# The first input of a decoder trunk: transposed as it was loaded, scaled while it is split

## The chip, the cores and the metric

The kernel runs on one core of one Trainium2 chip. TensorE does matrix products and transposes, VectorE and ScalarE work on tiles of 128 partitions, GpSimd does small things, and SyncE issues most loads. The metric is the device time of one execution in microseconds (us), lower is better.

## The reference

Two layers of a decoder, 256 tokens of width 1024, all in fp32. Each sub-layer is `x <- x + w * RMSNorm(f(RMSNorm(x)))`. The change touches only the start of the first one, whose f is a SwiGLU:

```python
def rms_norm(x, g):
    xf = x.astype(jnp.float32)
    y = xf * lax.rsqrt(jnp.mean(xf * xf, axis=-1, keepdims=True) + NORM_EPS)
    return (y * g.astype(jnp.float32)).astype(x.dtype)

def swiglu(x, w_in, w_out):
    gate, up = jnp.split(x @ w_in, 2, axis=-1)
    return (jax.nn.silu(gate) * up) @ w_out
```

w_in is 1024 x 5632, w_out 2816 x 1024. Five other sub-layers follow: a combined state-space and attention mixer, a recurrent mixer and three more SwiGLUs. None of their code is changed.

## The kernel before

**Precision.** Every fp32 operand of a large product is split into a high part (rounded to the format that TensorE streams fast) and a low part (what is left), and a product is made of three: high x high, high x low, low x high. ScalarE makes the high part by a copy, VectorE the low part by a subtraction. This is done for each piece of weights (`raw` to `w`, lines 252 and 253, in `prepare`) and for the input (`xT`, line 295, in `split_to`).

**Tiling.** Tokens come in two tiles of 128 (t = 0, 1). The input stands transposed in `xT`: 8 blocks of 128 channels, each with its high and low part for 256 tokens. The hidden width of 2816 is cut into 22 columns f, each with 128 gate and 128 up channels. For f = 0, 1, 2 the products go token tile by token tile (plan entries "A", `a_tile`, 16 products each: 8 wide ones of 512, 8 narrow ones of 256), after that both tiles together ("B"). The weights of a column come in two pieces of 512 KB. Four `raw` buffers hold pieces as loaded; a load waits until VectorE has split the piece that was in its buffer.

**The start.** `first_norms` lays out the start. The factor 1/rms of a token is not applied to the input; it is applied later to the hidden columns (`rs`, lines 548, 549 and 578), so only the weight of the norm, g, must reach the input before the products. Before, g was loaded as one row (`g_row`), spread over all partitions by products with a row of ones (`gain`, line 136), multiplied with the input on VectorE (`scaled`, line 396), transposed on TensorE (`flips`, line 140) and split, four blocks at a time (line 295). Five dummy products (`WARM`) on a tile of ones go ahead. `square` (line 390) sums the squares of a token tile's half on ScalarE, and GpSimd makes 1/rms of it (lines 302, 303). Tile 0 comes first; the two halves of tile 1 are transposed within the products of the first column (`second`).

**What sets the order.** TensorE's order is that in which the code calls it. ScalarE's and VectorE's order comes from a scheduler with priorities, but in `first_norms` it is fixed by hand: `turn` makes each instruction follow the one before it on its engine, and `weights(n)` puts the splitting of the next piece of weights into that row. Semaphores are set by the framework. It also makes instructions on different engines follow each other if they touch one bank of PSUM (the memory that TensorE writes; a tile called `rot` or `side` is one bank).

Of the kernel before, what the change touches and what calls it, by code (L numbers as in the profile page):

```python
# [8 lines left out]
F32 = mybir.dt.float32  # L9
# [3 lines left out]
ALU = mybir.AluOpType  # L13
# [3 lines left out]
P = 128  # L17
# [16 lines left out]
WARM = 5  # L34
# [78 lines left out]
def hybrid_trunk(ctx: ExitStack, tc: tile.TileContext, x_in, norm_g, ffn_in, ffn_out,  # L113
                 hyb_cols, hyb_v, hyb_dtf, conv_s, bias_dtf, a_log, d_rep, ssm_g, hyb_out,
                 rec_a, rec_cols, rec_vec, rec_wa, rec_wx, rec_out, out):
# [59 lines left out]
    g_row = begin.tile([P, DM], F32, name="g_row")  # L175
    act.dma_start(g_row[0:1, :], norm_g[0, 0:1, :])
# [87 lines left out]
    def halves(dst, ps):  # L264

        tmp = work.tile([P, 256], F32, name="half", bufs=2)
        act.copy(tmp, ps[:, 256:512])  # L267
        dve.tensor_tensor(dst, ps[:, 0:256], tmp, op=ALU.add)  # L268
# [107 lines left out]
    def first_norms(xT):  # L376
# [18 lines left out]
        def scaled(t, h):  # L395
            turn(dve.tensor_tensor(xg[t][:, h, :], xs[t][:, h * 512:(h + 1) * 512], gain[h], op=ALU.mult))

        def flips(t, h):
            ps = side()
            for k in range(4):  # L400
                flip(ps[:, k * P:(k + 1) * P], xg[t][:, h, k * P:(k + 1) * P])
            return ps.rearrange("p (k c) -> p k c", k=4), [xT[:, 4 * h:4 * h + 4, j, t * P:(t + 1) * P] for j in range(2)]
# [6 lines left out]
        def second():  # L409
            for h, lag in ((0, 0.5), (1, 1.0)):  # L410
                yield lag
                ps, dst = flips(1, h)
                turn(*split_to(dst[0], dst[1], ps))
            square(1, 0)
            square(1, 1)
            weights(4)
            hold[:] = latest.values()
            normed.add((0, 1))
            norms.discard((0, 1))

# [3 lines left out]
        gain, ms = [], []  # L424
        for t in range(NT):
            ms.append(work.tile([P, 2], F32, name="ms", bufs=4))
            rs.append(work.tile([P, 1], F32, name="r", bufs=4))
        slot = wp.tile([P, NT, 2, 512], F32, name="w", bufs=8)
        xg = [slot[:, t] for t in range(NT)]
        for h in range(2):  # L430
            gain.append(rot())
            mm(gain[h], ones[0:1, :], g_row[0:1, h * 512:(h + 1) * 512], True, True)
        square(0, 0)
        scaled(0, 0)
        scaled(0, 1)
        ps, dst = flips(0, 0)
        held = split_to(dst[0], dst[1], ps)
        turn(held[0])
        scaled(1, 0)
# [651 lines left out]
```

## Time and profile before

| | |
|---|---|
| median of 3 runs | 1053.39 us (1053.22 to 1054.23) |
| the profiled execution | 1052.26 us, of which the span is 1050.5 us |
| TensorE busy | 1037.0 us, 99% of the span |
| VectorE busy | 735.1 us, 70% |
| ScalarE busy | 600.3 us, 57% |

The span is the time from the first to the last instruction that the profile shows. PE is TensorE's product, PEld its loading of the stationary operand, DVE VectorE, ACT ScalarE, POOL GpSimd, SPq and ACTq the queues from which loads are issued. A row of the order of time gives start, duration, engine, line, operation, and in brackets how long the engine had been idle and what ended that. A product on fp32 operands shows as two records.

### The profile page before, as it was taken

To read this page: it belongs to the slowest core of one execution; us is meant where nothing else is said; L and a number is where in the kernel's file an instruction comes from. 1 tells how busy PE (TensorE), PEld (TensorE's weight loads), DVE (VectorE), ACT (ScalarE), POOL (GpSimd) and SP (SyncE) were. 2 spreads that over 40 slices of the span, in tenths; PEclk is the share of its full clock that TensorE was granted. 3 is DMA by queue.
4 is the path that set the end of the run, shared out by engine and by line. 5 is a ranking of instruction groups with operands and counts; after the bars stand their busy time and mean duration, and the time that the engine had idled before them with its cause. 6 is when DMAs were issued, how large, how long until landed. Compare 5 with 4: busy or idle time off the path is not lost.

```text
span 1050.5 us, 16060 instructions
## 1 busy us (share of the span) xinstructions
PE 1037.0 (99%) x6072; PEld 911.2 (87%) x6072; DVE 735.1 (70%) x1171; ACT 600.3 (57%) x1062; POOL 40.5 (4%) x78
## 2 busy tenths in 40 slices
PE   8999999999999999999999999999999999999997
PEld 6888888899999988888888888888889888888886
DVE  6876778589888766856567685666759878655563
ACT  5764555455565565655556474555659857554551
POOL 0011101100000001000000100000010010000000
PEclk9999999999999999999999999999999999999999
DMA  6886666366545563866567286566735356765521
GB/s 215 307 259 182 199 196 193 97 221 192 187 146 167 154 201 102 294 205 182 185 200 235 81 279 202 180 193 196 234 120 182 119 183 237 226 195 202 182 81 40
DMA packets 55699, 195.77 MB, mean 186 GB/s; under 512 B 6957, under 2 KB 8133, under 8 KB 55622
## 3 DMA queue, kind: packets, MB, share of 16 engines
q1 hardware_dynamic: 52416, 189.91, 56.2%
q10 hardware_dynamic: 3206, 4.84, 1.5%
q8 instruction: 47, 0.77, 0.3%
q14 instruction: 30, 0.25, 0.1%
HBM read 193.66 MB, written 1.07 MB: 185 GB/s over the span
## 4 chain that ended last, share of the span: by engine, by line
PE 74%; DVE 8%; DMA 7%; ACT 5%; issue 3%; POOL 1%; DVEq 0%; POOLq 0%; ACTq 0%; SPq 0%
PE rot L136 47%; PE side L136 26%; DMA raw<-in_ffn_out_dram 5%; DVE w L253 4%; ACT w L252 3%; DMA raw<-in_ffn_in_dram 2%; ACT junk L314 1%; PE rot L140 1%; DVE sg L268 1%; DVE xn L330 0%; POOL r L303 0%; DVE sc L966 0%; DVE x L365 0%; DVE sg L578 0%; ACT half L267 0%
## 5 line engine op out<-in xcount | busy, mean ns | idle before, releaser
L136 PE MATMUL rot<-xT,w 128*128 128x256 f32 (+1 forms) x3512 | 571.2, 321 | 0.0
L253 DVE TENSOR_TENSOR w<-raw,w 128x1024 fp32r<-128x1024 f32 (+1 forms) x350 | 431.2, 1235 | 190.0 <-ACT w L252 188.4
L136 PEld LDWEIGHTS rot<-xT,w 128*128 128x128 f32 x3512 | 504.3, 190 | 51.3 <-issue 1.3
L252 ACT CAST w<-raw 128x1024 fp32r<-128x1024 f32 (+1 forms) x350 | 364.7, 1047 | 159.9 <-DMA raw<-in_ffn_out_dram 121.1
L136 PE MATMUL side<-w,hid 128*128 128x512 f32 x1056 | 253.9, 390 | 0.3 <-ACT hid L295 0.3
L136 PEld LDWEIGHTS side<-w,hid 128*128 128x128 f32 x1056 | 197.2, 188 | 42.0 <-ACT hid L295 0.7
L136 PE MATMUL rot<-w,xT 128*128 128x256 f32 (+1 forms) x768 | 121.3, 316 | 2.1 <-DVE w L253 1.7
L136 PEld LDWEIGHTS rot<-w,xT 128*128 128x128 f32 x768 | 106.2, 192 | 12.0 <-DVE w L253 2.5
L295 ACT CAST hid<-up 128x256 fp32r<-128x256 f32 x76 | 30.9, 406 | 105.9 <-DVE up L583 105.7
L267 ACT COPY half<-rot 128x256 f32<-128x256 f32 x176 | 63.7, 362 | 9.6 <-PE rot L136 9.2
L295 DVE TENSOR_TENSOR hid<-up,hid 128x256 fp32r<-128x256 f32 x76 | 32.2, 424 | 27.7 <-ACT hid L295 27.7
L268 DVE TENSOR_TENSOR sg<-rot,half 128x256 f32<-128x256 f32 x100 | 41.8, 418 | 9.3 <-ACT half L267 9.3
L579 ACT ACTIVATE sg<-sg 128x256 f32<-128x256 f32 x76 | 31.7, 418 | 28.9 <-DVE sg L268 16.2
L136 PE MATMUL side<-w,os 128*128 128x512 f32 x192 | 46.2, 396 | 0.0
L136 PEld LDWEIGHTS side<-w,os 128*128 128x128 f32 x192 | 35.6, 188 | 7.9
L268 DVE TENSOR_TENSOR up<-rot,half 128x256 f32<-128x256 f32 x76 | 31.8, 419 | 4.3 <-ACT half L267 4.3
L302 POOL TENSOR_SCALAR r<-ms 128x1 f32<-128x1 f32 x24 | 7.2, 300 | 699.2 <-ACT junk L314 683.8
L583 DVE TENSOR_TENSOR up<-sg,up 128x256 f32<-128x256 f32 x76 | 31.8, 418 | 2.3 <-POOL up L582 1.5
L362 DVE TENSOR_TENSOR xn<-side,g_post 128x512 f32<-128x512 f32 x24 | 16.5, 691 | 17.9 <-ACT junk L314 17.5
L330 DVE SCALAR_TENSOR_TENSOR xn<-x,r,g_pre 128x512 f32<-128x512 f32 x20 | 14.2, 749 | 16.8 <-POOL r L303 16.8
L314 ACT ACTIVATE junk<-side 128x512 bf16<-128x512 f32 x24 | 14.3, 597 | 19.6 <-PE side L136 18.7
L314 ACT ACTIVATE junk<-x 128x512 bf16<-128x512 f32 x20 | 12.6, 631 | 19.4 <-DVE x L365 19.2
(197 smaller groups left out, 540.7 us busy)
## 6 DMA issues: line engine op xcount, KB each, us to landing
raw<-in_ffn_in_dram SPq DMA_DIRECT2D x176, 512.0 KB, 4.4
raw<-in_ffn_out_dram SPq DMA_DIRECT2D x88, 512.0 KB, 4.4
raw<-in_hyb_cols_dram SPq DMA_DIRECT2D x36, 512.0 KB, 4.1
raw<-in_hyb_out_dram SPq DMA_DIRECT2D x16, 512.0 KB, 3.6
raw<-in_hyb_v_dram SPq DMA_DIRECT2D x8, 512.0 KB, 4.1
raw<-in_rec_a_dram SPq DMA_DIRECT2D x8, 512.0 KB, 4.7
raw<-in_rec_cols_dram SPq DMA_DIRECT2D x8, 512.0 KB, 4.5
raw<-in_rec_out_dram SPq DMA_DIRECT2D x8, 512.0 KB, 3.6
```

The lines of the kernel that those rows point to most:

```text
L136: pe.matmul(ps, lhsT=lhsT, rhs=rhs, start=start, stop=stop)
L140: pe.transpose(ps, src, ident)
L252: splits.append(behind(act.copy(w[:, 0, c], raw[:, c]), hold))
L253: splits.append(behind(dve.tensor_tensor(w[:, 1, c], raw[:, c], w[:, 0, c].bitcast(F32), op=ALU.subtract), hold))
L267: act.copy(tmp, ps[:, 256:512])
L268: dve.tensor_tensor(dst, ps[:, 0:256], tmp, op=ALU.add)
L295: return act.copy(hi, src), dve.tensor_tensor(lo, src, hi.bitcast(F32), op=ALU.subtract)
L314: behind(act.activation(junk, src, func=AF.Square, scale=1.0 / (32.0 * weight), accum_out=ms[:, h:h + 1]), firsts)
L330: dve.scalar_tensor_tensor(xn[h], xt[:, cols], r, state["g_pre"][:, cols], op0=ALU.mult, op1=ALU.mult)
L362: behind(dve.tensor_tensor(hg[h], acc[h], state["g_post"][:, cols], op=ALU.mult), firsts)
L579: act.activation(sg, sg, func=AF.Silu)
L583: dve.tensor_tensor(up, sg, up, op=ALU.mult)
```

## The change

The input is transposed as it was loaded, and g, now loaded as a column of 8 values per partition, is a scale of the split: ScalarE's high part is `activation(scale=g)`, VectorE's low part is `src * g - high`. Since g differs from block to block, a split takes one block (128 x 128) and no longer four at once. All 16 transposes, of both token tiles, stand in a row ahead of the first product, with eight dummy products before them and four behind them. The order on ScalarE and VectorE is written out anew, and `halves` of the first columns gets an order behind it.

```diff
-WARM = 5
+WARM = 8
...
-    g_row = begin.tile([P, DM], F32, name="g_row")
-    act.dma_start(g_row[0:1, :], norm_g[0, 0:1, :])
+    g_cols = begin.tile([P, KT], F32, name="g_cols")
+    act.dma_start(g_cols, g_first)
...
-        def scaled(t, h):
-            turn(dve.tensor_tensor(xg[t][:, h, :], xs[t][:, h * 512:(h + 1) * 512], gain[h], op=ALU.mult))
-
         def flips(t, h):
             ps = side()
             for k in range(4):
-                flip(ps[:, k * P:(k + 1) * P], xg[t][:, h, k * P:(k + 1) * P])
-            return ps.rearrange("p (k c) -> p k c", k=4), [xT[:, 4 * h:4 * h + 4, j, t * P:(t + 1) * P] for j in range(2)]
+                flip(ps[:, k * P:(k + 1) * P], xs[t][:, (4 * h + k) * P:(4 * h + k + 1) * P])
+            return ps
+
+        def parts(t, h):
+            for k in range(4):
+                n, src = 4 * h + k, turned[t, h][:, k * P:(k + 1) * P]
+                hi, lo = (xT[:, n, j, t * P:(t + 1) * P] for j in range(2))
+                turn(act.activation(hi, src, func=AF.Identity, scale=g_cols[:, n:n + 1]))
+                turn(dve.scalar_tensor_tensor(lo, src, g_cols[:, n:n + 1], hi.bitcast(F32), op0=ALU.mult, op1=ALU.subtract))
...
+        turned = {(t, h): flips(t, h) for t in range(NT) for h in range(2)}
+        for _ in range(WARM // 2):
+            mm(warm[:, 0:P], ones, ones, True, True)
         square(0, 0)
...
+        parts(0, 0)
+        weights(1, 2)
+        parts(0, 1)
+        weights(2)
+        parts(1, 0)
+        parts(1, 1)
         square(0, 1)
...
+        state["ready"] = [list(latest.values())]
+        weights(4)
+        square(1, 0)
+        square(1, 1)
...
-                halves(sg, ps)
+                halves(sg, ps, state["ready"][t] if not ph else ())
...
+        "g_first": c(a["norm_g"][0, 0].reshape(KT, P).T),
```

The first place is ScalarE, from the first square to the cast of the second column's weights. Names: `junk` is a square, `side` a bank with four transposed blocks, `w` a piece of weights, `half` the copy that closes the first column's first token tile; the brackets say which semaphores an instruction waits for. Before:

```order
L295 CAST xT_98<-side_118 128x4x128 [waits PE_49]
L390 ACTIVATE junk_126,ms_105<-x0_83 128x512 [waits Activation_49]
L252 CAST w_132<-raw_130 128x512 [waits DMAHW3_49]
L252 CAST w_132<-raw_130 128x512
L295 CAST xT_98<-side_137 128x4x128 [waits PE_49]
L252 CAST w_146<-raw_144 128x1024 [waits DMAHW4_49]
L295 CAST xT_98<-side_159 128x4x128 [waits PE_49]
L295 CAST xT_98<-side_170 128x4x128 [waits PE_49]
L390 ACTIVATE junk_177,ms_107<-x1_84 128x512 [waits DMAHW2_49,Activation_49]
L390 ACTIVATE junk_179,ms_107<-x1_84 128x512 [waits Activation_49]
L267 COPY half_202<-rot_154 128x256 [waits PE_49]
L252 CAST w_185<-raw_183 128x1024 [waits DMAHW5_49]
```

Now, from the second group of parts on (the first, `side_112`, stands ahead of the first two rows in the same way):

```order
L252 CAST w_148<-raw_146 128x512 [waits DMAHW3_49]
L252 CAST w_148<-raw_146 128x512
L405 ACTIVATE xT_98<-side_117,g_cols_81 128x128 [waits PE_49]
L405 ACTIVATE xT_98<-side_117,g_cols_81 128x128 [waits DVE_49] x3
L252 CAST w_163<-raw_161 128x1024 [waits DMAHW4_49]
L405 ACTIVATE xT_98<-side_122,g_cols_81 128x128 [waits PE_49]
L405 ACTIVATE xT_98<-side_122,g_cols_81 128x128 [waits DVE_49] x3
L405 ACTIVATE xT_98<-side_127,g_cols_81 128x128 [waits PE_49]
L405 ACTIVATE xT_98<-side_127,g_cols_81 128x128 [waits DVE_49] x3
L390 ACTIVATE junk_182,ms_108<-x0_83 128x512 [waits Activation_49]
L267 COPY half_249<-rot_231 128x256 [waits PE_49]
L252 CAST w_188<-raw_186 128x1024 [waits DMAHW5_49]
```

Each cast of four blocks became four activations, of which the last three wait for VectorE (the value waited for is the count of the low part just before); all 16 stand ahead of the copy, and the two squares of tile 1 have moved behind the last row.

The second place is VectorE in the same stretch. Before:

```order
L396 TENSOR_TENSOR w_109<-x1_84,rot_110 128x512 [waits DMAHW2_49]
L295 TENSOR_TENSOR xT_98<-side_118,xT_98 128x4x128 [waits Activation_49]
L253 TENSOR_TENSOR w_132<-raw_130,w_132 128x512 [waits DMAHW3_49,Activation_49]
L253 TENSOR_TENSOR w_132<-raw_130,w_132 128x512 [waits Activation_49]
L295 TENSOR_TENSOR xT_98<-side_137,xT_98 128x4x128 [waits Activation_49]
L253 TENSOR_TENSOR w_146<-raw_144,w_146 128x1024 [waits DMAHW4_49,Activation_49]
L396 TENSOR_TENSOR w_109<-x1_84,rot_112 128x512
L295 TENSOR_TENSOR xT_98<-side_159,xT_98 128x4x128 [waits Activation_49]
L295 TENSOR_TENSOR xT_98<-side_170,xT_98 128x4x128 [waits Activation_49]
```

Now:

```order
L406 SCALAR_TENSOR_TENSOR xT_98<-side_112,g_cols_81,xT_98 128x128 [waits DMAHW0_49,Activation_49]
L406 SCALAR_TENSOR_TENSOR xT_98<-side_112,g_cols_81,xT_98 128x128 [waits Activation_49] x3
L253 TENSOR_TENSOR w_148<-raw_146,w_148 128x512 [waits DMAHW3_49,Activation_49]
L253 TENSOR_TENSOR w_148<-raw_146,w_148 128x512 [waits Activation_49]
L406 SCALAR_TENSOR_TENSOR xT_98<-side_117,g_cols_81,xT_98 128x128 [waits Activation_49] x4
L253 TENSOR_TENSOR w_163<-raw_161,w_163 128x1024 [waits DMAHW4_49,Activation_49]
L406 SCALAR_TENSOR_TENSOR xT_98<-side_122,g_cols_81,xT_98 128x128 [waits Activation_49] x4
L406 SCALAR_TENSOR_TENSOR xT_98<-side_127,g_cols_81,xT_98 128x128 [waits Activation_49] x4
```

The multiplications by g (`w_109`, a borrowed buffer) are gone, and each low part waits for the high part of its own block.

The third place is TensorE from its first instruction to the first column's second token tile. `rot_99` is the dummies' bank, `rot_154` and later `rot_231` the first token tile's sums. Before:

```order
L136 MATMUL rot_99<-ones_87 128x128 x5
L136 MATMUL rot_110<-g_row_81,ones_87 128x512
L136 MATMUL rot_112<-g_row_81,ones_87 128x512
L140 MATMUL side_118<-ident_91,w_109 128x128 x4
L140 MATMUL side_137<-ident_91,w_109 128x128 x4
L136 MATMUL rot_154<-w_132,xT_98 128x512
L136 MATMUL rot_154<-w_132,xT_98 128x256 x2
L136 MATMUL rot_154<-w_132,xT_98 128x512
L140 MATMUL side_159<-ident_91,w_109 128x128 x4
```

Now:

```order
L136 MATMUL rot_99<-ones_87 128x128 x8
L140 MATMUL side_112<-ident_91,x0_83 128x128 x4
L140 MATMUL side_117<-ident_91,x0_83 128x128 x4
L140 MATMUL side_122<-ident_91,x1_84 128x128 x4
L140 MATMUL side_127<-ident_91,x1_84 128x128 x4
L136 MATMUL rot_99<-ones_87 128x128 x4
L136 MATMUL rot_231<-w_148,xT_98 128x512
```

The transposes read the input as it was loaded (`x0`, `x1`), and the eight that stood between the first products have moved ahead of them.

## Rows read from the trace of the kernel before

**Rows 1.** The page: busy time by engine; the chain that ended last, by engine.

```profile
PE 1037.0 (99%) x6072; PEld 911.2 (87%) x6072; DVE 735.1 (70%) x1171; ACT 600.3 (57%) x1062; POOL 40.5 (4%) x78
PE 74%; DVE 8%; DMA 7%; ACT 5%; issue 3%; POOL 1%; DVEq 0%; POOLq 0%; ACTq 0%; SPq 0%
```

**Rows 2.** Stretches: from and to, length, busy time by engine, clock, DMA.

```profile
10.89:20.04 9.15, 9.15 (x40) 7.72 (x40) 6.05 (x9) 6.13 (x12) 0.87 (x2) 1.00 0.37 115
20.04:200.00 179.96, 179.65 (x957) 154.75 (x957) 133.72 (x190) 101.95 (x174) 18.62 (x23) 1.00 0.67 211
```

**Rows 3.** Order of time, 0 to 11 us: start, duration, engine, line, operation.

```profile
1.10 2.50 PE L136 MATMUL rot<-ones 128*128 128x128 f32 x10 [1.10 <-DVE power L298]
...
3.53 3.78 PE L136 MATMUL rot<-g_row,ones 1*128 1x512 f32 x4
4.49 0.63 ACT L390 ACTIVATE junk<-x 128x512 bf16<-128x512 f32 x1 [1.66 <-DMA x<-in_x_dram]
...
7.24 1.97 PE L140 MATMUL side<-ident,w 128*128 128x128 f32 x8
...
8.39 0.58 ACT L295 CAST xT<-side 128x512 fp32r<-128x512 f32 x1 [3.18 <-PE side L140]
...
9.01 0.69 DVE L295 TENSOR_TENSOR xT<-side,xT 128x512 fp32r<-128x512 f32 x1 [0.38 <-ACT xT L295]
...
9.50 1.12 ACT L252 CAST w<-raw 128x512 fp32r<-128x512 f32 x2
...
10.14 1.29 DVE L253 TENSOR_TENSOR w<-raw,w 128x512 fp32r<-128x512 f32 x2 [0.43 <-ACT w L252]
```

**Rows 4.** Order of time, 17 to 23 us.

```profile
17.43 0.35 ACT L267 COPY half<-rot 128x256 f32<-128x256 f32 x1
...
17.68 1.05 ACT L252 CAST w<-raw 128x1024 fp32r<-128x1024 f32 x1
...
18.76 1.23 DVE L253 TENSOR_TENSOR w<-raw,w 128x1024 fp32r<-128x1024 f32 x1 [0.53 <-ACT w L252]
...
20.04 2.65 PEld L136 LDWEIGHTS rot<-w,xT 128*128 128x128 f32 x16 [0.41 <-DVE w L253]
...
22.96 2.65 PEld L136 LDWEIGHTS rot<-w,xT 128*128 128x128 f32 x16
```

**Rows 5.** Loads: KB, us to landing; then the first weights' load: ns, start, landing.

```profile
x<-in_x_dram SPq DMA_DIRECT2D x2, 512.0 KB, 4.1
...
dsk<-in_d_rep_dram ACTq DMA_DIRECT2D x1, 4.0 KB, 1.7
...
L246 SPq DMA_DIRECT2D raw<-in_ffn_in_dram x1: 423/423/423, 1.7 to 1.7; - x1
DMA to landing us min/median/max: 5.3/5.3/5.3
```

**Rows 6.** ScalarE by form: shapes, count | busy us, mean ns | idle before.

```profile
L295 ACT CAST hid<-rot 128x128 fp32r<-128x128 f32 x24 | 6.4, 272 | 0.0
...
L545 ACT ACTIVATE h<-sg 128x128 f32<-128x128 f32 x18 | 5.6, 312 | 3.8 <-DVE sg L268 3.8
...
L947 ACT ACTIVATE sc<-side,hb 128x256 f32<-128x256 f32 x8 | 4.0, 496 | 0.1
...
L877 ACT ACTIVATE th<-rot 128x256 f32<-128x256 f32 x8 | 2.9, 380 | 11.1 <-PE rot L136 11.1
...
L548 ACT ACTIVATE h<-sg,r 128x128 f32<-128x128 f32 x6 | 2.4, 401 | 1.2 <-DVE sg L268 1.2
```

**Rows 7.** VectorE by form.

```profile
L295 DVE TENSOR_TENSOR hid<-rot,hid 128x128 fp32r<-128x128 f32 x24 | 6.7, 281 | 0.0
...
L549 DVE SCALAR_TENSOR_TENSOR h<-sg,r,h 128x128 f32<-128x128 f32 x6 | 2.1, 347 | 0.3 <-ACT h L548 0.3
```

**Rows 8.** TensorE by form, 13 to 14.2 us; then 16.6 to 19.7 us.

```profile
L136 PE MATMUL rot<-w,xT 128*128 128x512 f32 x2 | 1.1, 628 | 0.0
...
L136 PE MATMUL rot<-w,xT 128*128 128x512 f32 x11 | 2.9, 393 | 0.0
```

More of the change, by code (lines that the diff above doesn't have):

```diff
@@ L114, in hybrid_trunk @@
                  hyb_cols, hyb_v, hyb_dtf, conv_s, bias_dtf, a_log, d_rep, ssm_g, hyb_out,
-                 rec_a, rec_cols, rec_vec, rec_wa, rec_wx, rec_out, out):
+                 rec_a, rec_cols, rec_vec, rec_wa, rec_wx, rec_out, g_first, out):
     nc = tc.nc
@@ L262, in slabs, with halves @@
         return [split[k] for k in keys]
-    def halves(dst, ps):
+    def halves(dst, ps, firsts=()):
         tmp = work.tile([P, 256], F32, name="half", bufs=2)
-        act.copy(tmp, ps[:, 256:512])
-        dve.tensor_tensor(dst, ps[:, 0:256], tmp, op=ALU.add)
+        behind(act.copy(tmp, ps[:, 256:512]), firsts)
+        behind(dve.tensor_tensor(dst, ps[:, 0:256], tmp, op=ALU.add), firsts)
     def mm_wide(sums, groups):
@@ L407, in weights @@
             turn(*splits)
[L409 to L419, printed above, removed]
         warm = rot()
@@ L423, in first_norms @@
             mm(warm[:, 0:P], ones, ones, True, True)
[L424 to L432, printed above, removed]
-        square(0, 0)
[L434 to L439, printed above, removed]
-        turn(held[1])
-        square(0, 1)
-        weights(1, 2)
-        ps, dst = flips(0, 1)
-        turn(*split_to(dst[0], dst[1], ps))
-        weights(2)
-        scaled(1, 1)
-        normed.add((0, 0))
-        norms.add((0, 1))
+        ms = [work.tile([P, 2], F32, name="ms", bufs=4) for _ in range(NT)]
+        rs.extend(work.tile([P, 1], F32, name="r", bufs=4) for _ in range(NT))
+        turned = {(t, h): flips(t, h) for t in range(NT) for h in range(2)}
+        for _ in range(WARM // 2):
+            mm(warm[:, 0:P], ones, ones, True, True)
+        square(0, 0)
+        parts(0, 0)
[4 more added lines that the diff above has]
+        parts(1, 1)
+        square(0, 1)
+        state["ready"] = [list(latest.values())]
+        weights(4)
+        square(1, 0)
+        square(1, 1)
+        state["ready"].append(list(latest.values()))
+        hold[:] = latest.values()
+        normed.update({(0, 0), (0, 1)})
         start_pool.__exit__(None, None, None)
-        spawn(second())
     rs = []
```

## The prediction

> **What bounds the kernel now.** I read the page's first and fourth parts first. TensorE is busy for 99% of the span, and the chain that ended last lies on it for 74% [rows 1]. So a microsecond counts only if TensorE starts its dense work earlier or later, or waits inside it. The second view is TensorE's busy time by stretch: from 20.04 to 200 us it is 179.65 of 179.96 us [rows 2]. Behind 20.04 us this phase has almost nothing to gain, and almost no slack that could swallow a delay; what TensorE waits in later phases is for work that follows its own products and moves with it. The third view is the order of time up to 23 us [rows 3, 4]. Up to 20.04 us TensorE does five dummy products, the products that spread the norm's weight, 16 transposes and the two products of the first hidden column (token tiles 0 and 1). At 20.04 us the first product of the second hidden column starts (f = 1, tile 0). It had waited 0.41 us for VectorE's low part of its weights, which began at 18.76; ScalarE's high part of them began at 17.68, behind the copy at 17.43 [rows 4]. From there on one token tile follows another without a gap. **The end of the kernel therefore moves by as much as this 20.04 moves**, and 20.04 is set by the ScalarE and VectorE order ahead of it. I call the ScalarE cast of 17.68 the anchor: 2.36 us from it to 20.04.
>
> **The change: what goes and what is hidden.** The two products of the norm's weight, 3.78 us on TensorE, and four VectorE multiplications by it go [rows 3]. The transposes no longer wait for either and stand behind eight dummies. The small load of the weight by columns has 4 KB in 128 rows of 32 bytes; a load of the same form landed 1.7 us after its issue, the input's two loads take 4.1 [rows 5], so it is not last. The four dummies behind the transposes end at the latest at 5.0 + 2 x 1.97 + 4 x 0.49 = 10.9 us [rows 3]. The first product cannot start before 10.1 (below), and TensorE then waits on and off up to 20.8, so I cost them at nothing; without those waits it would be 0.8.
>
> **When the first parts can start.** Five dummies took 1.10 to 3.53, or 0.49 each [rows 3]; eight end at 1.10 + 8 x 0.49 = 5.0. The input's first tile is there at 4.49. From the first transpose to ScalarE's first cast went 8.39 - 7.24 = 1.15 us [rows 3]. So ScalarE starts the parts at **6.1** us instead of 8.39. That is the gain, 2.3 us at this place.
>
> **What it adds.** Four pairs of 128 x 512 (ScalarE high part, VectorE low part) become sixteen pairs of 128 x 128. The order of the program shows more: each ScalarE part but the first of a group waits for the VectorE part before it, and that one for ScalarE's. So the pairs do not overlap; one at a time goes to and fro. Behind a waiting part on ScalarE stand the casts of the next weights, and for those VectorE and then TensorE wait.
> Price of a ScalarE part: a cast of this size out of PSUM takes 272 ns; an activation with one column operand takes 401 against 312 without, and at 256 columns 496 against 380 [rows 6]. So 272 + 89 to 116 gives 361 to 388; the bounds are 272 and 401, and I take 380, nearer to the rows that read PSUM. Price of a VectorE part: 281 without a column operand, 347 with one [rows 7]; I take 345, the latter being the same operation. From one engine to the other went 0.03 us (17.68 + 1.05 is 18.73, VectorE started 18.76) [rows 4]. A pair is 0.38 + 0.345 + 2 x 0.03 = **0.785 us**, where the old pair of four times the width took 8.39 to 9.70, or 1.31 [rows 3]. Sixteen pairs in a row are 12.6 us, the four old ones 5.2.
>
> **The sum along the new order**, tile 0 first:
> Group 1, three pairs and the last high part: 6.1 + 3 x 0.785 + 0.38 = 8.84.
> First weights in two halves, VectorE 0.64 behind ScalarE and 1.29 long [rows 3]: 10.77. They landed at 7.0 [rows 5], so no wait.
> Group 2: its first low part stands behind those halves on VectorE; 0.345 + 0.03 + two pairs + 0.38: 13.09.
> Second weights, 1.05 on ScalarE, 0.03, 1.23 on VectorE [rows 4]: 15.40.
> Groups 3 and 4 (tile 1): 0.345 + three pairs gives 18.10 (ScalarE's first part of group 4 lies beside that), then 0.345 + 0.03 + two pairs + 0.38: 20.43.
> The square, 0.63 [rows 3], and the copy, 0.25 to the next [rows 4]: the anchor is at **21.3** instead of 17.68. With the same 2.36 us the second column starts at 23.66, that is **3.6 us later**. Seen from the other end: the pairs take 7.4 us more, the early start gives back 2.3 of it, and some 1.3 because the two squares of tile 1 (0.63 each) now stand behind the anchor.
> TensorE's own side: the first column's second product needs the last low part at 20.8 and has then one narrow and seven wide products left, some 1.8 of the 2.9 us of a token tile (20.04 to 22.96 [rows 4]): 22.6, before 23.66. So the weights stay last.
> Behind the anchor ScalarE has these two squares more. With the same durations the third column's (f = 2) two pieces of weights are whole 6.6 and 8.2 us behind the anchor; TensorE comes to them 2.36 + 2 x 2.92 = 8.2 us behind it, and needs the second piece later than the first. I cost the squares at nothing; without that cover they cost up to their 1.3.
>
> **The clock.** The column of the granted clock says 1.00 in the stretch from 10.89 to 20.04 [rows 2], but the rows of the products do not agree: the wide product took 628 ns between 13 and 14.2 us and 393 between 16.6 and 19.7 [rows 8], as the lower and the higher of its two levels (1.2 and 2.4 GHz) would. It rose between the two, among products and transposes in close order. In the new order TensorE has eight dummies, 16 transposes and four dummies in a row to about 10.9 us, and then 25 products spread up to 20.8. If the wide products are still slow at 20.8, the rest of the first column takes 3.6 us instead of 1.8 and ends at 24.4, 0.8 behind the weights, and each microsecond that the second column is slow costs half of it, say 0.3. Between 0 and 1.1 I take 0.4, since no row tells whether sparse products hold the clock. **Forecast: 4.0 us slower.**
> The profiled execution took 1052.26 us (span 1050.5) and would be 1056.3; it was 1.13 under the median of the runs, 1053.39, so the forecast for the median is 1057.4.
>
> **A rule that speaks against the change.** Each group's four transposes lie in one PSUM bank, and both parts are read from there. In the trace VectorE starts on the transposed tile only when ScalarE is done with it (9.01 behind 8.39 + 0.58 [rows 3]), but there it needs ScalarE's result anyway, so no run here shows that two readers shut each other out. The Trainium skill, PSUM — Partial Sum Buffer, section "PSUM bank collisions raise a hardware error", says that two engines must not be in one bank at once, reading included; by it these waits cannot be left out as long as a group shares a bank. By the rule the second column starts 3.6 us later; with parts that overlap it would be 2.4 us earlier (second rival).
>
> **Rivals.**
> *Cheap parts.* If a part costs what plain operations do, 272 and 281 ns [rows 6, 7], a pair is 0.61, and the same sum gives 1.35 us later; with a clock that rises during the dummies and the first part at 5.5, 0.75. For it: scale and low part may be free. Against: every row with a column operand is 66 to 116 ns longer. Time 1054.1 to 1054.8: not slower by what can be told.
> *The parts overlap.* If the waits cost nothing, ScalarE's own work decides: 6.1 + 16 x 0.38 + 1.12 + 1.05 [rows 3, 4] = 14.35, the square and the copy 0.88, 2.36: 17.6, or 2.4 us earlier than now, 1051.0. It decides as soon as a pair counts under 0.5 us. Against: the order holds a wait in both directions for each pair.
> *The clock stays low.* TensorE has only 25 products between 10.9 and 20.8 us, and the second column begins slow. To the 3.6 us come the 0.8 and half of what a wholly slow token tile loses (2.92 / 2), 2.2 in all: 5.8 later, 1059.2. It decides if the wide products still take over 600 ns when the second column starts. By the Trainium skill, TensorE: Matmul & The Clock Gate, Part 1, the slow state is the default and an idle engine falls back to it. The trace agrees so far that the wide product was slow again or still after the dummies and transposes [rows 8].
>
> **How the numbers follow.** A measurement of this kernel can tell about 0.2%, 2.1 us, from no change: slower is above 1055.5, faster under 1051.3. Forecast (3 to 5 us later) 0.58; cheap parts 0.16; overlap 0.05; low clock 0.21. So slower 0.79, within 0.2% 0.16, faster 0.05. The range 1054.4 to 1059.4 leaves out the overlap and the outer ends of the two others.
>
> **What the changed profile would show.** The first part on ScalarE near 6.1; high and low parts strictly in turn, 0.78 us a pair, the sixteenth low part near 20.8; weights of the second column on ScalarE near 21.3; its first product near 23.7 instead of 20.04, and behind it the same dense stream. I am wrong if pairs take under 0.65 us, if the wide products are fast all through the start and the parts come early, or if TensorE finds idle time behind 24 us that takes the delay in.

## The result, and the profile after

| | before | after |
|---|---|---|
| median | 1053.48 us (1053.22 to 1055.59) | 1062.26 us (1059.01 to 1064.98) |
| the profiled execution | 1052.26, span 1050.5 | 1064.98, span 1063.3 |
| TensorE busy | 1037.0 | 1037.6 |

The changed kernel takes 1.0074 times as long (95% interval 1.0048 to 1.01): slower, as forecast, but by 8.8 us and not by 4.0, and outside the range. The traced execution is the longest of its five; a second series of the same kernel gave 1.0059 (below).

The page of after, busy time by engine and the chain that ended last (of before: [rows 1]):

```profile
PE 1037.6 (98%) x6082; PEld 910.1 (86%) x6082; DVE 735.1 (69%) x1179; ACT 604.2 (57%) x1074; POOL 40.6 (4%) x78
PE 45%; DMA 22%; DVE 15%; ACT 10%; issue 6%; POOL 1%; DVEq 0%; POOLq 0%; ACTq 0%; SPq 0%
```

TensorE has 0.6 us more work in a span that is 12.8 us longer, so it waits. And the chain lies on loads for 22% instead of 7%. In before it leaves TensorE for long only in the first feed-forward phase (172 of the first 200 us); in after it also does so in the second and the fourth (146.5 of the 150 us from 430 on, 143 of the 155 from 880 on). There loads and the splitting of weights pace the span.

**The start.** TensorE of after in order of time (start, duration, ..., in brackets how long it had been idle and what ended that); before: [rows 3] and [rows 4].

```profile
1.10 3.58 PE L136 MATMUL rot<-ones 128*128 128x128 f32 x16 [1.10 <-DVE power L298]
4.68 2.29 PE L140 MATMUL side<-ident,x 128*128 128x128 f32 x16
6.80 1.06 PE L136 MATMUL rot<-ones 128*128 128x128 f32 x8
9.36 1.68 PE L136 MATMUL rot<-w,xT 128*128 128x512 f32 x8 [1.50 <-DVE w L253]
...
14.39 3.47 PE L136 MATMUL rot<-w,xT 128*128 128x512 f32 x10 [0.52 <-DVE w L253]
...
19.64 1.99 PE L136 MATMUL rot<-w,xT 128*128 128x256 f32 x8 [0.40 <-DVE xT L406]
22.33 0.85 PE L136 MATMUL rot<-w,xT 128*128 128x512 f32 x4 [0.71 <-DVE w L253]
```

The last row is the second column: 22.33 instead of 20.04, so 2.3 us later; 3.6 were forecast. ScalarE and VectorE there, the first two pairs and the anchor:

```profile
5.35 0.37 ACT L405 ACTIVATE xT<-side,g_cols 128x128 fp32r<-128x128 f32 x1
5.75 0.35 DVE L406 SCALAR_TENSOR_TENSOR xT<-side,g_cols,xT 128x128 fp32r<-128x128 f32 x1 [4.69 <-ACT xT L405]
6.13 0.37 ACT L405 ACTIVATE xT<-side,g_cols 128x128 fp32r<-128x128 f32 x1 [0.42 <-DVE xT L406]
6.54 0.35 DVE L406 SCALAR_TENSOR_TENSOR xT<-side,g_cols,xT 128x128 fp32r<-128x128 f32 x1 [0.44 <-ACT xT L405]
...
19.23 0.35 DVE L406 SCALAR_TENSOR_TENSOR xT<-side,g_cols,xT 128x128 fp32r<-128x128 f32 x1 [0.44 <-ACT xT L405]
...
19.96 1.06 ACT L252 CAST w<-raw 128x1024 fp32r<-128x1024 f32 x1
...
21.05 1.23 DVE L253 TENSOR_TENSOR w<-raw,w 128x1024 fp32r<-128x1024 f32 x1 [0.52 <-ACT w L252]
```

Each engine waits 0.42 to 0.44 us for the other, and a pair comes every 0.785 us (5.35, 6.13 and 6.92 on ScalarE): the pitch of the prediction.

**Where the rest arises.** From 22.33 us TensorE runs as densely as before for 140 us. The starts of its products, row by row against the rows of before, are later by a constant 2.57 us from 38 to 164 us, and then by steps: at the end of the first feed-forward phase (165 to 189 us) to 5.86, at the end of the second (552 to 571 us) to 10.6, of the fourth (1011 us) to 12.7; the third adds nothing, and the mixers in between 0.4 at most. This is one such step. Four rows of before, then seven of after, at the same place:

```profile
162.41 1.05 ACT L252 CAST w<-raw 128x1024 fp32r<-128x1024 f32 x1
163.42 0.42 DVE L268 TENSOR_TENSOR sg<-rot,half 128x256 f32<-128x256 f32 x1
163.89 1.52 PE L136 MATMUL side<-w,hid 128*128 128x512 f32 x6
165.25 5.73 PE L136 MATMUL rot<-xT,w 128*128 128x512 f32 x32
```

```profile
164.19 1.06 ACT L252 CAST w<-raw 128x1024 fp32r<-128x1024 f32 x1 [1.25 <-DMA raw<-in_ffn_out_dram]
...
166.46 1.52 PE L136 MATMUL side<-w,hid 128*128 128x512 f32 x6
167.02 1.05 ACT L252 CAST w<-raw 128x1024 fp32r<-128x1024 f32 x1 [1.78 <-DMA raw<-in_ffn_out_dram]
...
168.24 1.05 ACT L252 CAST w<-raw 128x1024 fp32r<-128x1024 f32 x1
169.19 0.38 ACT L267 COPY half<-rot 128x256 f32<-128x256 f32 x1
169.25 0.42 DVE L268 TENSOR_TENSOR sg<-rot,half 128x256 f32<-128x256 f32 x1
...
169.72 2.53 PE L136 MATMUL rot<-xT,w 128*128 128x512 f32 x16 [1.74 <-DVE sg L268]
```

Before, `sg` was written 1.4 us ahead of the products that need its place (163.84 against 165.25). After, ScalarE had waited 1.78 us for a load of `ffn_out`; two casts and the copy followed, and TensorE stood for 1.74 us. In these phases a load is issued when VectorE has emptied a `raw` buffer; it lands some 4 us later, is cast (1.05) and split (1.22), and this lets the next load go. From one cast of an `ffn_out` piece to the next the loop took 8.17 us in before (101.50 to 158.66 us, seven columns) and 8.61 in after. TensorE takes 8.29 us a column in the middle of a phase, but 6.93 in its last four (its out-steps start at 156.96, 163.89, 170.81 and 177.74 in before). There its lead over the loads is used up, and a loop that has fallen behind shows as idle TensorE: over those seven columns the loop of after lost 3.1 us against that of before (7 x 0.44).

So there were two questions: why the start costs 2.3 us, and why the loads' loop loses more in the changed kernel.

### The profile page after: what moved, and what is told of

The parts are those of the page before. It is cut to its first block, busy times and chain, and to the rows that moved or that the text cites. A ratio compares the mean times of both kernels' runs of the same rounds, so it can differ in the third digit from the quotient of the medians.

```text
span 1063.3 us, 16097 instructions
## 1 busy us (share of the span) xinstructions
PE 1037.6 (98%) x6082; PEld 910.1 (86%) x6082; DVE 735.1 (69%) x1179; ACT 604.2 (57%) x1074; POOL 40.6 (4%) x78
## 4 chain that ended last, share of the span: by engine, by line
PE 45%; DMA 22%; DVE 15%; ACT 10%; issue 6%; POOL 1%; DVEq 0%; POOLq 0%; ACTq 0%; SPq 0%
PE rot L136 27%; PE side L136 17%; DMA raw<-in_ffn_out_dram 17%; DVE w L253 8%; ACT w L252 6%; DMA raw<-in_ffn_in_dram 5%; DVE sg L268 2%; ACT junk L314 1%; DVE c L602 1%; PE rot L140 1%; DVE up L268 1%; ACT half L267 0%; DVE xn L330 0%; ACT xT L405 0%; POOL r L303 0%
## 5 line engine op out<-in xcount | busy, mean ns | idle before, releaser
L330 DVE SCALAR_TENSOR_TENSOR xn<-x,r,g_pre 128x512 f32<-128x512 f32 x20 | 14.2, 750 | 16.9 <-POOL r L303 16.9
```

The source lines that it names most:

```text
L330: dve.scalar_tensor_tensor(xn[h], xt[:, cols], r, state["g_pre"][:, cols], op0=ALU.mult, op1=ALU.mult)
```

## Experiments on the start

**The same kernel again.** 

> The changed kernel once more, beside the next three. Its second column started 2.3 us later than before, yet the median was 8.8 us longer. Theory 1 (place of the inputs): the 4 KB input that the change adds moves other inputs in memory, and the loads of weights take 0.1 to 0.5 us longer each; then this run again is 1059 to 1065. Theory 2 (the start alone): the late start throws the row of loads and splits out of step with TensorE in the phases behind it; the same 1059 to 1065. Theory 3 (chance of those runs): 1055.8.


1059.5 us, 1.0059 (1.0041 to 1.0077), second column at 22.40, steps at the same ends of phases but smaller (2.3, then 3.8, 5.2, 6.4). The loss is real, and it was 5.7 us in one series and 8.8 in the other.

**Two banks.** Neighbouring blocks of a token tile alternate between the two banks of that tile:

```diff
-                flip(ps[:, k * P:(k + 1) * P], xs[t][:, (4 * h + k) * P:(4 * h + k + 1) * P])
+                flip(ps[:, k * P:(k + 1) * P], xs[t][:, (2 * k + h) * P:(2 * k + h + 1) * P])
...
-        def parts(t, h):
-            for k in range(4):
-                n, src = 4 * h + k, turned[t, h][:, k * P:(k + 1) * P]
+        def parts(t, ns):
+            for n in ns:
+                src = turned[t, n % 2][:, n // 2 * P:(n // 2 + 1) * P]
```

> The changed kernel, but the blocks of a token tile lie in turn in two banks, so that ScalarE may work on the next block while VectorE is in the other bank. If the to and fro in one bank is what made the start long (0.79 us a pair), a pair now counts about 0.41, the second column starts near 18.2 us instead of 22.3, and the time falls by 4.1 against the changed kernel. If the parts themselves were the cost, it stays at 22.3. On the later stalls: theory 1 leaves them (about 1058 in all), theory 2 takes them away with the late start (about 1052).


1056.23 us, 1.0022 (1.0012 to 1.0031). The second column:

```profile
18.58 1.69 PE L136 MATMUL rot<-w,xT 128*128 128x512 f32 x10 [0.70 <-DVE w L253]
```

It starts 3.8 us earlier than with one bank and 1.5 earlier than in before. So the strict turn of the pairs comes from the waits that the framework sets for a shared bank, and costs 3.8 us here, where 4.1 were expected. But the kernel is still 2.4 us slower than before, although it starts earlier: the second question stands by itself.

**The new input.** Before with the 4 KB input declared but not read, and after without it (the first row of `norm_g` is stored in column order and read from its old place):

```diff
-    act.dma_start(g_cols, g_first)
+    act.dma_start(g_cols, norm_g[0, 0].rearrange("(p k) -> p k", k=KT))
```

> The kernel before, with the added input of 4 KB declared and never read; not one instruction differs. Theory 1 (place of the inputs): 1058 to 1061. Theory 2 (the start): as before, 1053.5. Theory 3: 1053.5.


1055.0 us, 1.0013 (1.0003 to 1.0022).


> The changed kernel without the added input: the same 4 KB by columns come from the norm's own tensor, whose first row is stored in that order. Theory 1 (place of the inputs): only the late start is left, 1053.5 + 2.3 = 1055.8. Theory 2 (the start): as the changed kernel, 1059 to 1065. Theory 3: 1055.8.


1059.68 us, 1.0056 (1.0042 to 1.0071), as much as with the input (1059.5). So the input accounts for 1.2 us at most, and without it the loss is the same.

**Before again, and before with a late start.** 

> The kernel before, unchanged, for a second profile of it. If the profile that the comparison rests on was an unusually good execution (1052.26 us against a median near 1053.8), this one loses 1 to 2 us at the ends of the feed-forward phases where TensorE then waits for the load loop, without any change at the start (second column at 20.0 us). If the kernel before simply never waits there, its later stretches agree within 0.5 us. Ratio 1.000 within 0.002 either way.


1053.55 us, 1.0004 (0.9995 to 1.0013); its second column started at 20.03. The execution on which the prediction's rows rest lost nothing at the ends of the phases; this one lost 1.1 us at the first. Two more traces of kernels whose medians lie near before's lost more at the end of the second: before_input 1.9 us, b_tail2 (below) 2.8.

```diff
+            for i in range(3):
+                junk = work.tile([P, 512], BF16, name="junk", bufs=1)
+                turn(act.activation(junk, xs[1][:, 0:512], func=AF.Square, accum_out=spare[:, i:i + 1]))
             weights(4)
```

> The kernel before, with three extra squares of 0.63 us (into an unread tile) on ScalarE ahead of the cast of the second column's weights. Nothing else is changed. The second column should start 1.9 to 2.8 us later, near 22 to 23 us, as late as in the changed kernel. Theory A (the late start by itself is paid back more than once, because TensorE's lead over the loads at the ends of the feed-forward phases is thin): about 5 to 6 us slower, near 1059. Theory B (a late start costs itself and no more, the rest comes from something else in the changed kernel): 1.9 to 2.8 us slower, 1055.5 to 1056.5.


1059.18 us, 1.0048 (1.0035 to 1.006). By the number it looks like theory A, but the trace says B:

```profile
22.95 4.61 PE L136 MATMUL rot<-w,xT 128*128 128x512 f32 x16 [2.67 <-DVE w L253]
```

The second column started 2.9 us later, and after 2.67 us of idleness its 16 products took 4.61 us instead of some 3.05: TensorE was at the lower of its two levels (granted clock 0.50 from 24 to 26 us). TensorE is then 4.4 us later, and at the end of the first phase 4.95: a late start does not multiply. (TensorE's columns also took 0.5% longer throughout, 0.04 us each, which no other run shows and which is not explained; this adds most of the rest of the 7.3 us by which its trace ends later.)

**The squares back.** The two squares of tile 1 ahead of the anchor, and no order on `halves`:

```diff
-        state["ready"] = [list(latest.values())]
-        weights(4)
         square(1, 0)
         square(1, 1)
-        state["ready"].append(list(latest.values()))
+        weights(4)
...
-                halves(sg, ps, state["ready"][t] if not ph else ())
+                halves(sg, ps)
```

> The changed kernel, with the two squares of the second token tile put back ahead of the cast of the second column's weights and no order behind the copies of the first columns. If a late start is what is paid, the second column starts 1.3 us later than in the changed kernel, near 23.7 us, and the time is 1.3 us or more above it, near 1061. If it is the new place of squares and copies behind the anchor that makes the later columns late, the time falls below the changed kernel's, to 1056 or 1058, though the second column starts later.


1062.16 us, 1.0081 (1.0066 to 1.0097): no faster, so the new place of the squares is not to blame. TensorE was 6.2 us later at 49 us, more than expected, and lost nothing at the end of the first phase. What this trace lost, 3.1 us, it lost at the place of 857 us in before, in front of the fourth phase: TensorE waited 1.99 us for `xn` there (0.22 in before), and the granted clock was 0.87 from 860 to 866 us and 0.84 from 866 to 872. The trace of b_tiny7 (below) has the same, 1.84 us and 3.1 in all. No experiment here is about that place.

## Experiments on the rest

**The dummies alone.** Before with eight dummies ahead, and four behind the transposes of tile 0:

```diff
-WARM = 5
+WARM = 8
...
         ps, dst = flips(0, 0)
+        for _ in range(WARM // 2):
+            mm(warm[:, 0:P], ones, ones, True, True)
```

> The kernel before, with the changed kernel's dummies alone: eight ahead, and four behind the first tile's transposes. If dummies only shift TensorE's clock, the products of the norm's weight run at the higher level and the second column starts within 0.5 us of 20.0; time 1053.3 to 1054.5. If the dummies delay the first products, the second column starts up to 1.5 us later, and so does the end: up to 1055.5.


1056.9 us, 1.0033 (1.0022 to 1.0044), although the second column starts 1.0 us earlier:

```profile
19.02 3.04 PE L136 MATMUL rot<-w,xT 128*128 128x512 f32 x16 [0.27 <-DVE w L253]
```

ScalarE, VectorE and the loads have the same order as in before, instruction for instruction. So dummies that cost no time at their place cost some 4 us later. In this trace one load of `ffn_out` (issued at 112.5; in before at 113.9) landed late while a 16 KB packet of the queue of instruction fetches went through the same DMA engines. The landing in before, the landing here, and the queue from 114 to 115 us (packets, MB, share of 16 engines):

```profile
DMA to landing us min/median/max: 3.7/3.7/3.7
```

```profile
DMA to landing us min/median/max: 5.5/5.5/5.5
```

```profile
q8 instruction: 1, 0.02, 9.8%
```

9.8% of 16 engines for 1 us is 1.6 us of one engine. In before this fetch came at 119.8, between two loads of `ffn_out`; more TensorE instructions at the start move each fetch against the columns. That became a theory (F): the place of the fetches. Four runs on it; in the first two, before gets seven or two small products behind the first transposes:

```diff
         ps, dst = flips(0, 0)
+        for _ in range(7):
+            mm(warm[:, 0:32], ones, ones[:, 0:32], True, True)
```

> The kernel before, with seven very small products (128x32, never read) on TensorE in the idle time of 1.7 us ahead of the first column. ScalarE, VectorE and the loads keep their order instruction for instruction. The second column should start within 0.2 us of 20.0. Theory F (what the changed kernel loses beyond its start is the place of TensorE's instruction fetches: each brings 16 KB through a load in flight, and more instructions ahead move them against the loads): the fetch that came at 119 us, between two loads of ffn_out, comes some 4 us earlier and falls into the load issued at 113.9; that load lands in 5 us or more instead of 3.7, and the kernel is 2 to 3.5 us slower, 1055.5 to 1057. Theory C (chance or the late start): no change, 1053 to 1054.3.


1059.7 us, 1.0048 (1.0031 to 1.0064); second column at 20.85, 0.8 later.


> As the run with seven small products, with two. By the theory of the fetches the one at 119 us comes 1 to 1.6 us earlier, at the very end of the load of ffn_out issued at 113.9 or behind it: little or no change, 1053 to 1055. By theory C no change, 1053 to 1054.3.


1053.79 us, 1.0 (0.9991 to 1.0008).

The other two are the changed kernel and the one with two banks, with seven dummies in all:

```diff
-WARM = 8
+WARM = 7
...
-        for _ in range(WARM // 2):
-            mm(warm[:, 0:P], ones, ones, True, True)
```

> The changed kernel with seven dummy products ahead of the transposes and none behind, so that TensorE has as many products ahead of the first column as the kernel before (five dummies and two for the weight of the norm), and its fetches fall against the columns as there. The second column should start near 22.4 us as in the changed kernel. By theory F the loss shrinks to about that of the start, 2.4 us: 1055.5 to 1057. By theory C it stays at 1059 to 1060.


1057.89 us, 1.0038 (1.0025 to 1.005). With only seven dummies the products behind 20 us ran at the lower level (24 of them in 7.48 us, granted clock 0.50 from 16 to 26 us), so TensorE is 4.3 us later at 49 us; but this is all: 4.1 at the end, and behind the start it waits nowhere in the first phase.


> The kernel whose neighbouring blocks lie in two banks, with the same seven dummies ahead and none behind. The second column should start near 18.6 us, 1.5 earlier than in the kernel before. By theory F it is 2 us or more below the run with eight and four dummies (1056.2), level with the kernel before or a little faster: 1052 to 1054. By theory C it stays near 1056.


1052.15 us, 0.9984 (0.9975 to 0.9994): 1.7 us under before, in one series. The pairs overlap, the second column starts at 18.02, and the chain leaves the loads:

```profile
5.72 1.59 ACT L405 ACTIVATE xT<-side,g_cols 128x128 fp32r<-128x128 f32 x4 [0.23 <-PE side L140]
...
6.12 1.57 DVE L406 SCALAR_TENSOR_TENSOR xT<-side,g_cols,xT 128x128 fp32r<-128x128 f32 x4 [5.07 <-ACT xT L405]
...
18.02 3.07 PE L136 MATMUL rot<-w,xT 128*128 128x512 f32 x16 [0.72 <-DVE w L253]
```

```profile
PE 87%; DVE 6%; ACT 4%; issue 1%; DMA 1%; POOL 1%; DVEq 0%; POOLq 0%; ACTq 0%
```

All four moved to the side that theory F names, b_tiny7 and a_equal further up than it says. But the slow and the fast among them differ in the length of TensorE's program too, so length itself was a rival.

**Place or length.** In a_wide the changed kernel's twelve dummies are six of twice the width; a_many has twelve small products (128x32) instead of the four behind; b_tail7 has before's seven small products behind TensorE's last product, where they move no fetch (the one at 119.8 us in before came at 120.0). First a_wide, then b_tail7:

```diff
-        for _ in range(WARM):
-            mm(warm[:, 0:P], ones, ones, True, True)
+        wide = ones.unsqueeze(1).to_broadcast([P, 2, P])
+        for _ in range(WARM // 2):
+            mm(warm[:, 0:2 * P].rearrange("p (a b) -> p a b", a=2), ones, wide, True, True)
...
     for ph in range(len(PHASES)):
         xT = run(ph, xT)
+    tail = rot()
+    for _ in range(7):
+        mm(tail[:, 0:32], ones, ones[:, 0:32], True, True)
```

> The changed kernel with its twelve dummy products of 128 columns put together to six of 256: the same time on TensorE, but six instructions fewer, so that its instruction fetches fall against the columns where they fall in the kernel before (near 119 us plus the shift, not 116). The second column should start at 22.3 to 22.6 us as in the changed kernel. Fetch theory: only the start is paid, 2.3 to 2.6 us, and the time is 1055.5 to 1057. Late start or chance: 1059 to 1061, as the changed kernel.


1057.52 us, 1.0042 (1.0027 to 1.0058); 3.3 us later at 49 us (the lower level here too, 0.50 from 22 to 24 us), 4.6 at the end.


> The changed kernel with twelve products of 128x32 behind the transposes in place of four of 128x128. A dummy moved the fetch by about 0.6 us against the columns (eight instructions more: 119.8 to 114.9); eight more move it from 116.0 to about 111, which is 8.3 us, one column, ahead of the place in the kernel before, so between the loads of ffn_out again. Fetch theory: the loss beyond the start goes although TensorE has yet more instructions, 1055.5 to 1057.5 with the second column at 22.3 to 22.8. If the number of instructions or where the program lies in memory is what counts: 1059 or more.


1058.83 us, 1.0056 (1.0041 to 1.0071); 2.9 us later at 49 us, 6.2 at the end.


> The kernel before, with the seven small products of the earlier run behind TensorE's last product instead of ahead of the first column: the program is as much longer, and no fetch ahead of the end moves. Fetch theory: no change, 1053 to 1054.5. If the length of the program or the place in memory is what counts: 1057 to 1060, as with the seven at the start.


1056.12 us, 1.0029 (1.0017 to 1.0042).
The last two speak against F and for the length. But the traced execution of b_tail7 (1052.63 us) had lost nothing, so three more runs:


> The kernel before with seven small products behind TensorE's last product, once more: the first series gave 3.0 us more than the kernel before, though its profiled execution (1052.63 us) lost nothing anywhere. If the longer program is what makes the loads land later, the ratio is 1.002 to 1.004 again and a profile of an execution near the median shows the loss at the ends of the feed-forward phases, where TensorE waits for weights. If the first series was chance: ratio 1.000 within 0.001.


1058.18 us, 1.0045 (1.0029 to 1.006).


> Two small products behind the last one. So far programs with up to 3 more TensorE instructions than the kernel before lost 0 to 2 us beyond their start and those with 7 to 15 more lost 3 to 6. If the length is what counts, this one is level with the kernel before, 1052.5 to 1054.5. If any product behind the last one costs time by itself: 1055 to 1057.


1053.21 us, 0.9998 (0.9986 to 1.0011).


> Twenty small products behind the last one, 2.3 us of TensorE time that ends before the results are written. If a longer program costs, once a size is passed: 3 us again, 1056 to 1058. If the products at the end cost by themselves, about three times what seven do: 1061 or more. If the first series was chance: 1053 to 1054.5.


1057.12 us, 1.0035 (1.0017 to 1.0053).
**This decides it.** Seven or twenty small products behind TensorE's last one, beside the final norm, cost 3 to 5 us, two cost nothing, and twenty no more than seven. ScalarE, VectorE, GpSimd and the loads run the same instructions in the same order in all of them, and in b_tail20's trace TensorE's last product ahead of the twenty is already 2.7 us late. The chain, first of b_tail7 in its second trace, then of b_tail20:

```profile
PE 46%; DMA 21%; DVE 14%; ACT 9%; issue 6%; POOL 1%; DVEq 0%; POOLq 0%; ACTq 0%; SPq 0%
```

```profile
PE 49%; DMA 21%; DVE 15%; ACT 9%; issue 6%; POOL 1%; ACTq 0%; SPq 0%; DVEq 0%; POOLq 0%
```

These are the changed kernel's shares. Not every trace of a longer program has them (b_dummies and b_tiny7 kept 71% on TensorE, b_tail7's first trace 87%), and a short one can come near (before_input 62%). The wait of TensorE at the end of the fourth phase in b_tail7's second trace (995 to 1035 us), and of the second in b_tail20 (540 to 600), in total, times, longest:

```profile
PE rot L136 <- DVE sg L268: 1.5, 1, 1.5
```

```profile
PE rot L136 <- DVE sg L268: 1.2, 1, 1.2
```

It is the wait that after has at these places (1.3 and 1.9 us). But b_tail2's one trace has it too, 1.9 us at the end of the second phase, and its median is level with before. So a trace shows where the time goes, and the medians decide whether it does.

The runs in one table. The bytes are 64 for each record of TensorE in the trace and 256 more; some 250 records, 16 KB, lie between two fetches. "Start" is how much later than in before TensorE is at the out-step of 49 us in the one trace, less 0.55, the mean of the seven traces whose kernels leave the start as it was (0 to 1.0); "rest" is the difference of the medians less that.

| kernel | TensorE's program, bytes | start | time | rest |
|---|---|---|---|---|
| a_wide | 781,184 | +2.7 | +4.5 | 1.7 |
| before_input | 781,312 | +0.4 | +1.2 | 0.8 |
| b_late | 781,312 | +3.8 | +5.6 | 1.8 |
| a_equal | 781,440 | +3.8 | +4.0 | 0.2 |
| two_equal | 781,440 | -2.3 | -1.7 | 0.6 |
| b_tail2 | 781,824 | -0.4 | -0.1 | 0.3 |
| b_tiny2 | 781,888 | +1.5 | -0.1 | -1.6 |
| after | 782,720 | +2.0 | +8.8 | 6.8 |
| after_again | 782,720 | +1.8 | +5.7 | 3.9 |
| after_no_input | 782,720 | +2.5 | +5.8 | 3.4 |
| after_two_banks | 782,720 | -1.6 | +2.4 | 4.0 |
| a_squares | 782,784 | +5.6 | +8.6 | 3.0 |
| b_tail7, b_tail7_again | 783,104 | +0.4, +0.1 | +3.1, +4.9 | 2.6, 4.8 |
| b_dummies | 783,168 | -1.3 | +3.3 | 4.6 |
| b_tiny7 | 783,168 | +0.5 | +5.8 | 5.4 |
| a_many | 784,768 | +2.3 | +5.8 | 3.4 |
| b_tail20 | 786,432 | -0.2 | +3.8 | 4.0 |

Up to 781,888 bytes the rest is -1.6 to 1.8 us, from 782,720 on 2.6 to 6.8. Two series of one kernel differ by 2 to 3 us (after, b_tail7), so the two groups are told apart by all of their members and not by any one; where between them the edge lies was read from the table afterwards. What differs in the traces is the landing of the loads, by little: in the dense stretches of the four feed-forward phases (loads issued at 40 to 160, 445 to 550, 630 to 735 and 900 to 1005 us) the mean load of `ffn_out` landed 4.37 us behind its issue in the nine traces of the first kind, before's two among them (4.29 to 4.49), and 4.50 in the eleven of the second (4.39 to 4.60); of `ffn_in` 4.09 against 4.18. Some 17 to 20 columns a phase, each 0.13 us longer, would be 2 to 3 us (an estimate), which is the size of a step.

**What stays open** is by what way a longer program makes the loads land later. One thing goes with the edge: the longer programs need one more block of 16 KB. Up to 781,888 bytes the traces hold 47 fetches of TensorE's program and from 783,104 on 48; at 782,720 two of the four hold the 48th just behind the last instruction, and the other two, and a_squares, hold 47. It comes at 1041 us or later, behind all the steps, so this fetch itself does not delay those loads. That something moves in memory with the longer program is a guess that no run here tests. Nor does it cost in every execution: b_tail7's first trace lost nothing (its mean was 4.40).

## Why the prediction was wrong

- **The pair, 0.785 us:** right to the hundredth; 0.37 on ScalarE and 0.35 on VectorE (0.38 and 0.345 were put in). By form, 4 to 20 us:

```profile
L405 ACT ACTIVATE xT<-side,g_cols 128x128 fp32r<-128x128 f32 x16 | 5.8, 368 | 6.4 <-DVE xT L406 6.3
L406 DVE SCALAR_TENSOR_TENSOR xT<-side,g_cols,xT 128x128 fp32r<-128x128 f32 x16 | 5.5, 350 | 9.9 <-ACT xT L405 9.9
```

- **Strictly in turn, for the shared bank:** right. The turn is one of waits that the framework sets. Between turn and overlap lie 3.8 us (4.3 in two_equal) and not the 6.0 of the sum and the second rival. The prediction set the Trainium skill, PSUM — Partial Sum Buffer, section "PSUM bank collisions raise a hardware error" beside this. The run with two banks agrees as far as it goes: pairs in different banks overlap, at 0.40 us a pair (1.59 for four). What two engines in one bank at once would do no run here shows.
- **The start, +3.6:** the sign and the way right, the size 2.3. Two terms were too large. The first part started at 5.35 and not at 6.1, since the transposes ran at the higher level already: 16 in 2.29 us, where eight took 1.97 in [rows 3]. And the rest of the chain was 0.6 us shorter than the sum of its durations, largely because ScalarE's rows overlap by some 0.1 us (7.71 + 0.37 is 8.08, the next cast started at 7.97). From the anchor to TensorE it was 2.37, as put in.
- **The clock, +0.4:** the doubt was right, the price here nil: the second column waited for its weights. The granted clock was 0.83 from 10 to 20 us (start and end, length, busy by engine, clock, DMA) and 1.00 before the second column began:

```profile
10.00:20.00 10.00, 6.39 (x24) 4.52 (x24) 5.08 (x13) 5.58 (x16) 0.10 (x1) 0.83 0.33 113
20.00:24.00 4.00, 3.29 (x19) 2.58 (x18) 3.12 (x5) 3.97 (x10) 1.04 (x3) 1.00 0.18 35
24.00:200.00 176.00, 173.13 (x917) 147.87 (x916) 129.25 (x184) 98.88 (x167) 18.39 (x23) 1.00 0.67 215
```

  The rival "the clock stays low" did come, in other kernels: in a_equal and b_late products of the second column ran at the lower level, and this cost 1.5 to 2 us.
- **"I cost them at nothing", of the dummies: the step that failed.** At their place they cost nothing, as said; the +3.3 us of b_dummies come elsewhere. The sum had a term for the time of an added instruction and none for its being there. By the table this makes 3.9 to 6.8 of the changed kernel's 5.7 to 8.8 us; with six or five products fewer (a_wide, a_equal) the change keeps its late start and 1.7 or 0.2 us of rest. That the length of the program is what does it the runs show; by what way stays open. So the late start alone, some 2 us of median, is about half of the 4.0 forecast, and the range was left through a term that it did not have (the second series, 1059.5, lies just above its upper end).
- **"Almost no slack that could swallow a delay; what TensorE waits in later phases ... moves with it":** half right. In the short programs a shift of the start goes through to the end (a_equal 4.3 us at 49 us and 4.1 at the end, two_equal -1.8 and -1.1). But TensorE's later starts are set in part by the loads' loop, which can fall behind by itself. The hint stood in [rows 1]: the chain lay on TensorE for 74%, and I did not ask where the other 26% were. Two thirds of them are in the first feed-forward phase: followed back from a wait of 0.3 us at its end, the chain runs through loads and splits for the whole phase. So the margin was nearly used up there already.
- The last of its own warning signs, idle time of TensorE behind 24 us, is what happened (the last row above: 173.13 of 176.00 busy), but to add to the delay and not to take it in.

## What to carry to other kernels

A busy share of 99% says little about the places where the margin is thin: follow the chain to each stretch where it leaves the bound engine, for there a tenth of a microsecond per load adds up. Two engines that read one tile in small pieces go to and fro if the framework makes them take turns at a shared bank (0.785 us a pair here); alternate two banks (0.40). And a difference of a few us can come, as here, from the mere length of a program: before a part of a change is blamed, run the kernel before with that many instructions more where they do nothing.

## What the runs showed of the hardware that I had not expected

- TensorE's program comes in during the run, 16 KB at a time, some 23 us apart in the dense stretches, through the DMA engines that the loads use. Below, the queue in before and in b_tail7 (packets, MB, share):

```profile
q8 instruction: 47, 0.77, 0.3%
```

```profile
q8 instruction: 48, 0.79, 0.3%
```

  The Trainium skill, Runtime: NRT & Kernel Launch, section "Instruction fetch mechanics", gives the same block and calls the cost mostly hidden. For TensorE itself the trace of before agrees: eight fetches from 20.04 to 200 us, and 179.65 of 179.96 us busy. For the loads the traces do not: in the dense stretches of 20 traces, 171 loads of `ffn_out` with a fetch in their flight landed after 4.78 us in the mean, 827 without after 4.37. But b_tail7 and a_many show that this is not what the changed kernel paid, and without a fetch in flight the two kinds of programs still differ (4.32 and 4.41).
- A longer TensorE program alone (the same work, 1,792 bytes more) cost 3.0 and 4.9 us of 1053, about 0.4%, with an edge between 781,888 and 782,720 bytes.
- Executions of one kernel differ by up to 6 us: the two traces of after end 6.3 us apart, those of b_tail7 4.0, nearly all of it from the ends of phases. One trace shows where time can be lost, and only the medians whether it is.
- The column of the granted clock reads 1.00 where the trace has no record of the clock. In before the first record, 1.0, stands at 16.13 us; so the 1.00 of [rows 2] from 10.89 us on is no reading up to there, and the prediction was right to go by the products (628 ns, then 393). In b_late and a_equal wide products took 628 ns at a recorded 0.50.
